# Two-layer token mixer on one core: mixtures, taps and norm moved beside the sparse heads, new rates for the Strassen groups

## The chip, the cores and the metric

The kernel runs on one core of one Trainium2 chip. The metric is the device time of one execution in microseconds (us), as the median of several runs. The core's engines are named as the profile names them: PE is the matrix engine, PEld its weight load, DVE the vector engine, ACT the scalar engine, POOL and SP the two others, of which SP issues most transfers and POOL the paced ones.

## The reference, cut to what matters

Two layers (D_MODEL 2048, 256 tokens) each normalise the input, multiply it by one wide matrix, run three mixers on the parts, gate them, project each back and add them under sigmoid gates:

```
h = rms_norm(x, norm_w)
proj = h @ w_in          # (256, 2048) @ (2048, IN_WIDTH)
(qa, ka, va, za, qi, ki, wi, ub, zb, qc, kc, vc, zc, gates) = split(proj)
y_a = (dsa_attention(rope(qa), rope(ka), va, rope(qi), rope(ki), wi, top_k) * silu(za)) @ w_a_out
y_b = (conformer_conv(ub, conv_w, conv_b, cln_w, cln_b) * silu(zb)) @ w_b_out
y_c = (stick_breaking_attention(qc, kc, vc) * silu(zc)) @ w_c_out
g = sigmoid(gates).reshape(b, s, 3, D_MODEL)
x + (g[..., 0, :] * y_a + g[..., 1, :] * y_b + g[..., 2, :] * y_c) @ w_out
```

All data are float32. The convolution has 31 taps per channel and is followed by a layer norm.

## The kernel before, in words

**Units.** Weights come from DRAM in pieces of 512 KB (256 rows by 512 columns), called units here; SP issues each load (L276) into one of six buffers `raw`. Each float32 operand is split in two numbers that the fast matrix mode takes: ACT rounds the unit (L287, `wh`), DVE subtracts to get the rest (L292, `wl`), with three buffers for each. PE then makes twelve matmuls for the unit (L303), eight with `wh` and four with `wl`. A chunk of 512 output columns is eight units in one PSUM tile (`acc`).

**Strassen groups.** Part of the merge gates (`gates`, four of the six column pairs named in `FAST`, L38) is computed by a Strassen scheme, `strassen`, one group after the other. A group works through "products" of six matmuls each, four with `wh` and two with `wl`, but each still wants a whole L287 and L292; 20 products make up its first part, with three sums of operands per five products (L1205, DVE), and eight its second. A group holds two tiles `mm` and one half of an `acc` tile: the banks o1 and o7 are in one `mm` tile. Between the parts the first results are read out of PSUM: L1256 (ACT), L1257 to L1260 (DVE); L1259 reads o7. The second part then adds on to o1 and o7 and ends in L1271 and L1272.

**What sets the order.** The emission order is made by Python generators at build time. After every unit, `background` (L156) advances the generators in two lists, `turns` and `stages`: at most `pace` and `wide` of them, sorted by rank and due time. The taps of the convolution are in a list of their own that gives one tap every `every` units. `combine` (L1135) yields the rest of the projection and the three back projections (za, zb, two `early` chunks, w_b, w_c, w_a); for each unit it adds RATES[kind] to a debt `owed`, and as long as `stages` is empty the debt is paid with items of the Strassen groups (one item is about a product). In `stages` are the indexer's two parts, four sparse heads, `conv_norm` (the layer norm of the convolution) and `mixtures` (L1070s to L1090s: DVE forms four sums of the activations for the groups, L1081 and L1089, and splits them, L416 and L417). Groups cannot start before all of these are done.

**Turns.** A gating that needs its data with rows and columns exchanged goes through `turn_in`: ACT copies the words apart (L180), SP issues two transposing DMAs (L186, the tuple `turn` says after how many units), DVE and ACT copy the words back (L194, L196), and a DVE chain (L447, L456) ends it. LATE is the tuple of the two za and the two zb gatings of a layer.

**Parked parts.** Half-done activations of w_c and w_a lie in DRAM (`parked`) and come back through POOL, one paced transfer after the other (L254, L256).

Of the kernel before, what the change touches and what calls it, by code (L numbers as in the profile page):

```python
# [12 lines left out]
ALU = mybir.AluOpType  # L13
# [16 lines left out]
EPS = 1e-6  # L30
NEG = -1e30
TAKEN = -3e38
RATES = (2.35, 2.35, 2.35, 2.35)
TURN = (8, 8)
EARLY = (4, 6)
LATE = (6, 6)
MERGED = ((3, 7), (3, 6), (3, 5))
FAST = ((2, 0), (2, 1), (0, 0), (0, 1))  # L38
SCALE = float(128 ** -0.5)
# [14 lines left out]
def trunk(ctx: ExitStack, tc: tile.TileContext, x, xt, w_in, w_a, w_b, w_c, w_out,  # L54
# [45 lines left out]
    def big():  # L100
        return [slot(), slot()]
# [34 lines left out]
    def t4(dt=F32):  # L136
        return tp.tile([P, 1024], dt, tag="t4", bufs=8, name=nm("t4"))
# [36 lines left out]
    def turn_in(src, dst, then=None, slots=True, turn=TURN, early=False):  # L174
        own, cols = words(slots)
        rows = own.rearrange("p (t w d) -> p t w d", t=NT, w=2)
        s16 = src.bitcast(U16).rearrange("p t (d w) -> p t d w", w=2)
        with tc.high_priority():
            for i in range(2):
                nc.scalar.copy(rows[:, :, i, :], s16[:, :, :, i])  # L180

        def steps():
            yield turn[0]
            with tc.high_priority() if turn in MERGED else nullcontext():
                for t in range(NT):
                    nc.sync.dma_start(cols.rearrange("p (g t) -> p g t", g=8)[:, :, t * P:(t + 1) * P],  # L186
                                      own[:, t * 1024:(t + 1) * 1024], transpose=True)
            yield turn[1]
            halves_ = cols.rearrange("p (w f t) -> p w f t", w=2, f=4)
            into = own.bitcast(F32).rearrange("p (f t) -> p f t", f=4) if dst is None else dst  # L190
            d16 = into.bitcast(U16).rearrange("p f (t w) -> p f t w", w=2)
            bound = turn == LATE or turn in MERGED
            with tc.issue_after(lows[0].ins) if bound else nullcontext(), tc.high_priority() if bound else nullcontext():
                nc.vector.tensor_copy(d16[:, :, :, 1], halves_[:, 1])  # L194
            with tc.issue_after(highs[0].ins) if bound else nullcontext(), tc.high_priority() if bound else nullcontext():
                (nc.vector.tensor_copy if early else nc.scalar.copy)(d16[:, :, :, 0], halves_[:, 0])  # L196
            more = None
            if dst is None:
                more = then(into, cols.bitcast(F32).rearrange("p (f t) -> p f t", f=4))
            elif then is not None:  # L200
                more = then()
            if hasattr(more, "send"):
                yield from more

        entry = [steps(), count[0], lambda: True, 0]
        turns.append(entry)
        advance(entry)
        return entry

    def start(gen, ready=lambda: True, rank=0):  # L210
        stages.append([gen, 0, ready, rank])
        return stages[-1]
# [5 lines left out]
    every = [1]  # L218
    pace = [1]
# [310 lines left out]
    for layer in range(DEPTH):  # L530
# [408 lines left out]
        def index_far(qb2=qb2, ki=ki, wi=wi, bias=bias):  # L939
            cb = cst[:, C_CB:C_CB + S]  # L940
            sc = tp.tile([P, S], F32, tag="sc", bufs=2, name=nm("sc"))
            bs = tp.tile([P, S], F32, tag="bias", bufs=2, name=nm("bias"))
            for g in range(NIH // 4):
                ps = mm_tile()
                complete(rotated[g])
                for q in range(4):
                    for n, (i, j) in enumerate(three):
                        nc.tensor.matmul(ps[:, q * S:(q + 1) * S], qb2[i][:, g * 4 + q, :], ki[:, j, 0, :],  # L948
                                         start=n == 0, stop=n == 2)
                rl = t4()  # L950
                nc.scalar.activation(rl, ps, AF.Relu)
                yield 1
                for q in range(4):
                    hd = g * 4 + q
                    nc.vector.scalar_tensor_tensor(sc, rl[:, q * S:(q + 1) * S], wi[:, 1, hd:hd + 1],
                                                   cb if hd == 0 else sc, op0=ALU.mult, op1=ALU.add)
            yield 1
            yield from chosen(sc, bs, cb)
            bias[1] = bs

        every[0] = 3
        start(index_far())
# [2 lines left out]
        def early_steps(b, j):  # L965
            a = yield from chunk_steps(w, [(O_G + b * D + j * 512, 512)], hx, KD)
            sg_ = t4().rearrange("p (t d) -> p t d", t=NT)
            with tc.high_priority():
                for t in range(NT):
                    nc.scalar.activation(sg_[:, t, :], a[t], AF.Tanh, scale=0.5)  # L970
            nc.gpsimd.dma_start(gates[b][:, :, j * 512:(j + 1) * 512].rearrange("t p d -> p t d"), sg_)  # L971
# [104 lines left out]
        def mixtures():  # L1076
            for h in range(2):
                f = []
                for u in range(2):
                    v = t4().rearrange("p (k t) -> p k t", k=4)  # L1080
                    nc.vector.tensor_add(v, hx[2 * u + h][:, :, 0, :].bitcast(F32), hx[2 * u + h][:, :, 1, :].bitcast(F32))  # L1081
                    f.append(v)
                (a11, a21), (a12, a22) = ((v[:, :, :P], v[:, :, P:]) for v in f)
                m1, m2 = (t4().rearrange("p (n k t) -> p n k t", n=2, k=4) for _ in range(2))
                yield 1
                for n, (o, x_, y_, op) in enumerate((
                        (m1[:, 0], a21, a22, ALU.subtract), (m1[:, 1], m1[:, 0], a11, ALU.subtract),
                        (m2[:, 0], a12, m1[:, 1], ALU.add), (m2[:, 1], a11, a21, ALU.subtract))):
                    nc.vector.tensor_tensor(o, x_, y_, op=op)  # L1089
                    split(mix[n][:, 4 * h:4 * h + 4, 0, :], mix[n][:, 4 * h:4 * h + 4, 1, :], o)  # L1090
                    yield 1

        start(mixtures(), rank=1)
        pace[0] = 2
        gated = {2: gate(O_ZC, qcT, [], w, hx, park=parked[2], slots=(True, False))}
        gated[0] = []
        za = gate_steps(O_ZA, qaT, [], w, hx, gated[0], park=parked[0], slots=(False, False), turn=LATE, need=sparse)
# [37 lines left out]
        def combine():  # L1135
            kind[0] = 2
            yield from za
            yield from early_steps(1, 2)
            yield from early_steps(1, 3)
            finish()  # L1140
            pace[0], wide[0] = 1, 2
            yield from zb
            mg.extend(v.rearrange("p a b -> p (a b)").rearrange("p (j t d) -> p j t d", j=2, t=NT) for v in big())
            for e in gated[1]:
                complete(e)
# [68 lines left out]
        def strassen(b, jj):  # L1214
# [50 lines left out]
            for u in range(4):  # L1265
                product(o1, plain(0, KC), u, halves(block(KC, 0, u)), True)
                yield 1
                product(o7, plain(1, KC), u, halves(kept[u]), True)
                yield 1
            with tc.high_priority():  # L1270
# [159 lines left out]
```

## Time and profile before

| | |
|---|---|
| runs, not profiled | 2059.34 us median of 3 (2058.57 to 2060.51) |
| the profiled execution | 2063.1 us, span in its trace 2061.2 us |
| PE busy | 2004.9 us, 97% of the span |
| DVE busy | 1650.7 us, 80% |
| ACT busy | 1435.9 us, 70% |
| POOL busy | 212.8 us, 10% |
| transfers | 475.39 MB, mean 231 GB/s |

The share of an engine is an average over stages that have different limits, so the table says which engine is full in most of them, not what ends a wait in one of them. The profiled execution's own time is 1.9 us above its span and 3.8 us above the median of the other runs. Times in the trace are in us from the start of its span.

### The profile page before, as it was taken

To read this page: it belongs to the slowest core of one execution; us is meant where nothing else is said; L and a number is where in the kernel's file an instruction comes from. 1 tells how busy PE (TensorE), PEld (TensorE's weight loads), DVE (VectorE), ACT (ScalarE), POOL (GpSimd) and SP (SyncE) were. 2 spreads that over 40 slices of the span, in tenths; PEclk is the share of its full clock that TensorE was granted. 3 is DMA by queue.
4 is the path that set the end of the run, shared out by engine and by line. 5 is a ranking of instruction groups with operands and counts; after the bars stand their busy time and mean duration, and the time that the engine had idled before them with its cause. 6 is when DMAs were issued, how large, how long until landed. Compare 5 with 4: busy or idle time off the path is not lost.

```text
span 2061.2 us, 27065 instructions
## 1 busy us (share of the span) xinstructions
PE 2004.9 (97%) x9470; PEld 1679.4 (81%) x9470; DVE 1650.7 (80%) x1792; ACT 1435.9 (70%) x2056; POOL 212.8 (10%) x252
## 2 busy tenths in 40 slices
PE   9999999999889989999999999999998899899998
PEld 7888889988668867887888888899886687778877
DVE  8688777897988777886676888788989887788765
ACT  7699877668766655565657997776787656565753
POOL 0000000000212113410000000000002211144000
PEclk9999999999999999999999999999999999999999
DMA  8787657669799889998977775586696998899973
GB/s 279 214 227 208 186 156 223 204 181 232 200 255 277 232 238 283 313 301 234 266 196 221 212 213 172 165 230 187 197 242 180 276 282 223 244 296 310 310 235 126
DMA packets 353145, 475.39 MB, mean 231 GB/s; under 512 B 109680, under 2 KB 167792, under 8 KB 352880
## 3 DMA queue, kind: packets, MB, share of 16 engines
q1 hardware_dynamic: 322688, 412.43, 68.5%
q0 software_dynamic: 28864, 58.73, 11.6%
q10 hardware_dynamic: 1456, 2.51, 0.4%
q8 instruction: 74, 1.21, 0.2%
q14 instruction: 63, 0.52, 0.1%
HBM read 423.79 MB, written 23.07 MB: 217 GB/s over the span
## 4 chain that ended last, share of the span: by engine, by line
PE 85%; DVE 5%; ACT 3%; DMA 3%; issue 2%; SPq 0%; POOL 0%; ACTq 0%; DVEq 0%; POOLq 0%
PE acc L303 73%; PE mm L303 9%; ACT wh L287 2%; DVE wl L292 2%; DMA t<-t 2%; DVE t L1205 1%; DVE s L1205 1%; DMA raw<-in_w_in_dram 1%; PE mm L948 1%; PE mm L978 1%; DMA s<-parked 0%; PE mm L1018 0%; PE mm L813 0%; PE mm L769 0%; ACT t L180 0%
## 5 line engine op out<-in xcount | busy, mean ns | idle before, releaser
L303 PE MATMUL acc<-wh,s 128*128 128x512 f32 (+2 forms) x4352 | 1071.5, 387 | 16.6 <-ACT wh L287 11.0
L292 DVE TENSOR_TENSOR wl<-raw,wh 128x1024 fp32r<-128x1024 f32 (+2 forms) x698 | 838.3, 1207 | 289.5 <-ACT wh L287 271.3
L287 ACT CAST wh<-raw 128x1024 fp32r<-128x1024 f32 (+2 forms) x697 | 723.6, 1040 | 394.3 <-PE acc L303 302.7
L303 PEld LDWEIGHTS acc<-wh,s 128*128 128x128 f32 x4352 | 804.0, 188 | 185.9 <-ACT wh L287 16.5
L303 PE MATMUL acc<-wl,s 128*128 128x512 f32 (+2 forms) x2176 | 576.1, 385 | 4.4 <-DVE wl L292 4.4
L303 PEld LDWEIGHTS acc<-wl,s 128*128 128x128 f32 x2176 | 403.8, 188 | 87.6 <-DVE wl L292 6.7
L303 PE MATMUL mm<-wh,s 128*128 128x512 f32 x768 | 214.7, 399 | 20.9 <-ACT wh L287 16.0
L482 ACT ACTIVATE t<-s,cst 128x255 f32<-128x255 f32 (+14 forms) x480 | 201.5, 489 | 0.1
L303 PEld LDWEIGHTS mm<-wh,s 128*128 128x128 f32 x768 | 145.2, 191 | 60.5 <-ACT wh L287 24.9
L254 POOL COPY sm<-sm 128x3 f32<-128x3 f32 x108 | 110.3, 1045 | 391.7 <-ACT sm L253 391.7
L485 DVE TENSOR_TENSOR s<-s,t 128x1020 f32<-128x1020 f32 (+14 forms) x120 | 138.5, 1154 | 2.0 <-ACT t L482 1.3
L303 PE MATMUL acc<-s,wh 128*128 128x384 f32 (+1 forms) x608 | 126.4, 348 | 0.0
L303 PE MATMUL mm<-wl,s 128*128 128x512 f32 x384 | 121.0, 396 | 4.6 <-DVE wl L292 4.3
L971 POOL DMA_DIRECT2D gates<-t x8 | 6.0, 752 | 1026.8 <-ACT t L970 1026.8
L303 PEld LDWEIGHTS acc<-s,wh 128*128 128x128 f32 x608 | 104.3, 189 | 3.1
L287 ACT CAST wh<-t 128x1024 fp32r<-128x1024 f32 x64 | 67.0, 1048 | 50.9 <-PE acc L303 16.2
L287 ACT CAST wh<-s 128x1024 fp32r<-128x1024 f32 x64 | 67.1, 1049 | 50.7 <-DVE s L1205 32.5
L292 DVE TENSOR_TENSOR wl<-s,wh 128x1024 fp32r<-128x1024 f32 x64 | 78.2, 1222 | 18.4 <-ACT wh L287 16.6
L292 DVE TENSOR_TENSOR wl<-t,wh 128x1024 fp32r<-128x1024 f32 x64 | 78.3, 1223 | 17.8 <-ACT wh L287 16.6
L303 PEld LDWEIGHTS mm<-wl,s 128*128 128x128 f32 x384 | 72.6, 191 | 23.7 <-DVE wl L292 8.9
L303 PEld LDWEIGHTS acc<-s,wl 128*128 128x128 f32 x608 | 79.2, 191 | 1.0
L303 PE MATMUL acc<-s,wl 128*128 128x192 f32 (+1 forms) x608 | 79.7, 273 | 0.0
(248 smaller groups left out, 1361.8 us busy)
## 6 DMA issues: line engine op xcount, KB each, us to landing
raw<-in_w_in_dram SPq DMA_DIRECT2D x554, 512.0 KB, 4.5
raw<-in_w_out_dram SPq DMA_DIRECT2D x64, 512.0 KB, 5.0
s<-in_w_in_dram POOLq DMA_DIRECT2D x32, 512.0 KB, 9.1
raw<-in_w_b_dram SPq DMA_DIRECT2D x32, 512.0 KB, 5.5
raw<-in_w_c_dram SPq DMA_DIRECT2D x32, 512.0 KB, 6.7
raw<-in_w_a_dram SPq DMA_DIRECT2D x32, 512.0 KB, 7.1
t<-gates POOLq DMA_DIRECT2D x20, 512.0 KB, 7.0
s<-parked POOLq DMA_DIRECT2D x32, 256.0 KB, 6.4
```

The lines of the kernel that those rows point to most:

```text
L254: seen = nc.gpsimd.tensor_copy(copy[:, :3], mark)
L287: highs[0] = nc.scalar.copy(u[1], u[0])
L292: sub = nc.vector.tensor_sub(u[2], u[0], u[1].bitcast(F32))
L303: newest[0] = nc.tensor.matmul(o, lhsT, rhs, start=start, stop=stop, skip_group_check=True)
L482: nc.scalar.activation(o[:, i, :S - d], yT[:, c, :S - d], AF.Copy, scale=wq)
L485: sums.append(lambda: nc.vector.tensor_add(to, to, o[:, :, :S - d]))
L948: nc.tensor.matmul(ps[:, q * S:(q + 1) * S], qb2[i][:, g * 4 + q, :], ki[:, j, 0, :], start=n == 0, stop=n == 2)
L971: nc.gpsimd.dma_start(gates[b][:, :, j * 512:(j + 1) * 512].rearrange("t p d -> p t d"), sg_)
L978: nc.tensor.matmul(ps[:, q * n:(q + 1) * n], qaT[:, c * 4 + q, ts_], kaT[:, c, :n], start=True, stop=True)
L1205: nc.vector.tensor_tensor(o, a_, b_, op=op)
```

## The change

Five things change. (1) `mixtures` forms its sums in place in the four operand tiles and asks for no further buffers; it starts as soon as the indexer's second part has ended, with rank 0, ahead of the sparse heads, and from there on `pace` is 3 (was 2), `wide` 6 (was 4) and `every` 1 (was 3), so that the rest of the taps comes with every unit. (2) RATES is 2.15 for kind 2 (za, zb and early) and 2.5 for kinds 0 and 1 (the back projections); it was 2.35. (3) The transposing DMAs of LATE are emitted with high priority, and the wait of units behind them is 8 (was 6). (4) The two `early` chunks stand behind zb (were ahead of it), and `finish()` ahead of zb. (5) The second part of a group makes its four o1 products and then its four o7 products (they alternated).

```diff
-RATES = (2.35, 2.35, 2.35, 2.35)
+RATES = (2.5, 2.5, 2.15, 2.5)
-LATE = (6, 6)
+LATE = (6, 8)
...
-            with tc.high_priority() if turn in MERGED else nullcontext():
+            with tc.high_priority() if turn == LATE or turn in MERGED else nullcontext():
...
             bias[1] = bs
+            bias["far"] = True
...
-                m1, m2 = (t4().rearrange("p (n k t) -> p n k t", n=2, k=4) for _ in range(2))
...
-                        (m1[:, 0], a21, a22, ALU.subtract), (m1[:, 1], m1[:, 0], a11, ALU.subtract),
-                        (m2[:, 0], a12, m1[:, 1], ALU.add), (m2[:, 1], a11, a21, ALU.subtract))):
+                        (a22, a21, a22, ALU.subtract), (a22, a22, a11, ALU.subtract),
+                        (a12, a12, a22, ALU.add), (a21, a11, a21, ALU.subtract))):
...
-        start(mixtures(), rank=1)
-        pace[0] = 2
+        start(mixtures(), lambda: "far" in bias, 0)
+        pace[0], wide[0], every[0] = 3, 6, 1
...
             yield from za
-            yield from early_steps(1, 2)
-            yield from early_steps(1, 3)
             finish()
             pace[0], wide[0] = 1, 2
             yield from zb
+            yield from early_steps(1, 2)
+            yield from early_steps(1, 3)
...
                 product(o1, plain(0, KC), u, halves(block(KC, 0, u)), True)
                 yield 1
+            for u in range(4):
                 product(o7, plain(1, KC), u, halves(kept[u]), True)
                 yield 1
```

Three places in the order of instructions follow, all of layer 0 (layer 1 is the same). The first is PE where the first Strassen group runs. In these rows `mm_5100`, `mm_5101` and `acc_5102` are the group's banks before, and `mm_4876`, `mm_4877` and `acc_4878` after; `acc_4832` is a chunk of 512 columns. Before:

```order
L303 MATMUL mm_5100<-wh_5243,s_9_100 128x512 x4
L303 MATMUL mm_5101<-wh_5253,s_686_4130 128x512
L303 MATMUL mm_5100<-wl_5244,s_9_100 128x512 x2
L303 MATMUL mm_5101<-wh_5253,s_686_4130 128x512 x3
L303 MATMUL mm_5101<-wl_5254,s_686_4130 128x512 x2
L303 MATMUL mm_5101<-wh_5267,s_687_4131 128x512 x4
L303 MATMUL acc_5102<-wh_5279,s_688_4132 128x512 x2
L303 MATMUL mm_5101<-wl_5268,s_687_4131 128x512 x2
L303 MATMUL acc_5102<-wh_5279,s_688_4132 128x512 x2
L303 MATMUL mm_5100<-wh_5294,s_689_4133 128x512
L303 MATMUL acc_5102<-wl_5280,s_688_4132 128x512 x2
L303 MATMUL mm_5100<-wh_5294,s_689_4133 128x512 x3
```

After:

```order
L303 MATMUL acc_4832<-wh_4994,s_10_101 128x512 x8
L303 MATMUL acc_4832<-wl_4995,s_10_101 128x512 x4
L303 MATMUL mm_4876<-wh_5014,s_8_99 128x512 x4
L303 MATMUL mm_4876<-wl_5015,s_8_99 128x512 x2
L303 MATMUL mm_4877<-wh_5024,s_686_4130 128x512 x4
L303 MATMUL mm_4877<-wl_5025,s_686_4130 128x512 x2
L303 MATMUL acc_4832<-wh_5039,s_10_101 128x512 x8
L303 MATMUL acc_4832<-wl_5040,s_10_101 128x512 x4
L303 MATMUL mm_4877<-wh_5057,s_687_4131 128x512 x4
L303 MATMUL mm_4877<-wl_5058,s_687_4131 128x512 x2
L303 MATMUL acc_4832<-wh_5070,s_11_102 128x512 x8
L303 MATMUL acc_4832<-wl_5071,s_11_102 128x512 x4
```

Before, products follow products (six matmuls each) without a unit between them; after, a unit of twelve matmuls stands behind every one or two of them.

The second place is DVE at the end of the first part of the fourth group, while w_a is being multiplied; `acc_7792` before and `acc_7762` after is w_a's first chunk, and L1169 multiplies it by its merge gate. Before:

```order
L292 TENSOR_TENSOR wl_7902<-raw_7899,wh_7901 128x1024
L1257 TENSOR_TENSOR t_1532_7872<-mm_7244,t_1532_7872 128x512
L1258 TENSOR_TENSOR t_1533_7873<-mm_7244,t_1532_7872 128x512
L292 TENSOR_TENSOR wl_7912<-s_1396_7311,wh_7911 128x1024
L1259 TENSOR_TENSOR t_1533_7873<-t_1533_7873,mm_7243 128x512
L1260 TENSOR_TENSOR t_1533_7873<-acc_7245,t_1533_7873 128x512
L1169 SCALAR_TENSOR_TENSOR t_1513_7786<-t_1513_7786,acc_7792 128x1024
L292 TENSOR_TENSOR wl_7937<-raw_7935,wh_7936 128x1024
L292 TENSOR_TENSOR wl_7956<-raw_7953,wh_7955 128x1024
L292 TENSOR_TENSOR wl_7966<-s_1423_7432,wh_7965 128x1024
L1173 TENSOR_TENSOR s_1173_6405<-s_1173_6405,t_1513_7786 128x1024
```

After:

```order
L292 TENSOR_TENSOR wl_7923<-raw_7921,wh_7922 128x1024
L1257 TENSOR_TENSOR t_1531_7886<-mm_7313,t_1531_7886 128x512
L1258 TENSOR_TENSOR t_1532_7887<-mm_7313,t_1531_7886 128x512
L1169 SCALAR_TENSOR_TENSOR t_1502_7756<-t_1502_7756,acc_7762 128x1024
L292 TENSOR_TENSOR wl_7942<-raw_7939,wh_7941 128x1024
L1173 TENSOR_TENSOR s_1150_6340<-s_1150_6340,t_1502_7756 128x1024
L1259 TENSOR_TENSOR t_1532_7887<-t_1532_7887,mm_7312 128x512
L1260 TENSOR_TENSOR t_1532_7887<-acc_7314,t_1532_7887 128x512
```

L1169, the subtraction behind it and L1173 now stand between L1258 and L1259; before, one subtraction stood there, and L1169 came behind L1260. On PE the chunk's last matmuls stand directly ahead of the first product of the group's second part in the order after, which asks for L1259.

The third place is DVE at the last gating of zb: its back copy L194, then the chain L447 and L456 that writes the second half of what w_b multiplies by. Before, `raw_6479`, `raw_6509` and `raw_6558` are units of w_b; their subtractions stand among the gating's operations:

```order
L292 TENSOR_TENSOR wl_6481<-raw_6479,wh_6480 128x1024
L292 TENSOR_TENSOR wl_6498<-s_1193_6477,wh_6497 128x1024
L1205 TENSOR_TENSOR t_1199_6507<-raw_6397,raw_6475 128x1024
L292 TENSOR_TENSOR wl_6511<-raw_6509,wh_6510 128x1024
L194 COPY t_1171_6401<-t_1172_6402 128x1024
L292 TENSOR_TENSOR wl_6528<-raw_6475,wh_6527 128x1024
L447 SCALAR_TENSOR_TENSOR t_1171_6401<-t_1172_6402,s_81_537 128x1024
L292 TENSOR_TENSOR wl_6543<-t_1199_6507,wh_6542 128x1024
L1205 TENSOR_TENSOR t_1211_6556<-raw_6552,raw_6554 128x1024
L292 TENSOR_TENSOR wl_6560<-raw_6558,wh_6559 128x1024
L292 TENSOR_TENSOR wl_6577<-raw_6552,wh_6576 128x1024
L456 TENSOR_TENSOR s_1176_6417<-t_1171_6401,s_1176_6417 128x4x256
```

After, the same three operations of this gating stand among units of the early chunks and the second group, and the first unit of w_b is the twelfth row behind this piece:

```order
L194 COPY t_1027_5766<-t_1028_5767 128x1024
L292 TENSOR_TENSOR wl_6119<-raw_6091,wh_6118 128x1024
L292 TENSOR_TENSOR wl_6129<-t_1100_6095,wh_6128 128x1024
L1205 TENSOR_TENSOR s_1109_6140<-t_1100_6095,raw_6138 128x1024
L292 TENSOR_TENSOR wl_6144<-raw_6142,wh_6143 128x1024
L447 SCALAR_TENSOR_TENSOR t_1027_5766<-t_1028_5767,s_81_537 128x1024
L292 TENSOR_TENSOR wl_6162<-s_1109_6140,wh_6161 128x1024
L1205 TENSOR_TENSOR t_1115_6171<-raw_6093,raw_6138 128x1024
L292 TENSOR_TENSOR wl_6175<-raw_6173,wh_6174 128x1024
L292 TENSOR_TENSOR wl_6194<-raw_6138,wh_6193 128x1024
L292 TENSOR_TENSOR wl_6210<-raw_6208,wh_6209 128x1024
L456 TENSOR_TENSOR s_1119_6191<-t_1027_5766,s_1119_6191 128x4x256
```

Before, w_b's first unit stands eleven rows ahead of L194; after, w_b's first unit stands 23 rows behind it.

## Rows read from the trace of the kernel before

**Rows 1.** The page: busy time, share and instructions; chain by engine.

```profile
PE 2004.9 (97%) x9470; PEld 1679.4 (81%) x9470; DVE 1650.7 (80%) x1792; ACT 1435.9 (70%) x2056; POOL 212.8 (10%) x252
...
PE 85%; DVE 5%; ACT 3%; DMA 3%; issue 2%; SPq 0%; POOL 0%; ACTq 0%; DVEq 0%; POOLq 0%
```

**Rows 2.** Windows: engines' busy time (count of instructions), PEclk, DMA share, GB/s.

```profile
450.00:500.00 50.00, 50.00 (x223) 41.52 (x222) 37.81 (x42) 43.74 (x79) 0.00 (x0) 1.00 0.86 222
500.00:550.00 50.00, 50.00 (x223) 41.39 (x222) 48.45 (x59) 40.61 (x47) 1.52 (x2) 1.00 0.82 211
545.00:612.00 67.00, 54.57 (x211) 40.34 (x211) 59.65 (x58) 43.29 (x54) 21.21 (x13) 0.95 0.83 228
715.00:760.00 45.00, 38.42 (x154) 29.38 (x152) 34.93 (x33) 27.42 (x36) 13.42 (x16) 0.92 0.85 227
...
1565.00:1635.00 70.00, 57.20 (x229) 42.59 (x229) 63.92 (x62) 47.91 (x59) 20.86 (x13) 0.98 0.85 227
1738.00:1785.00 47.00, 40.66 (x165) 30.96 (x164) 36.72 (x33) 27.92 (x33) 12.46 (x15) 0.96 0.89 234
```

**Rows 3.** Groups by line and shape on DVE: busy us, mean ns, idle before.

```profile
L292 DVE TENSOR_TENSOR wl<-raw,wh 128x1024 fp32r<-128x1024 f32 x678 | 824.1, 1222 | 271.7 <-ACT wh L287 257.8 <-ACT t L779 10.0
...
L1205 DVE TENSOR_TENSOR t<-raw,raw 128x1024 f32<-128x1024 f32 x64 | 77.9, 1218 | 0.0
...
L1169 DVE SCALAR_TENSOR_TENSOR t<-t,acc 128x1024 f32<-128x1024 f32 x16 | 19.5, 1218 | 4.6 <-PE acc L303 4.6
...
L1259 DVE TENSOR_TENSOR t<-t,mm 128x512 f32<-128x512 f32 x8 | 5.4, 680 | 0.0
```

**Rows 4.** The chain that ended last, 545 to 612: start, us, what.

```profile
590.49 2.72 PE acc L303 x12
...
600.04 1.06 ACT wh L287
601.13 1.23 DVE wl L292
602.36 0.61 DVE t L1259
```

**Rows 5.** Waits of PE: us in total, times, longest us.

```profile
PE mm L303 <- DVE t L1259: 4.9, 3, 2.2
```

**Rows 6.** The chain that ended last, 715 to 760: start, us, what.

```profile
722.44 1.82 ACT t L180 x2
...
725.62 8.39 DMA t<-t
...
734.10 0.75 DVE t L194
...
736.40 2.93 PE acc L303 x6
...
756.76 1.36 PE mm L303 x6
```

**Rows 7.** Groups by line and shape on ACT.

```profile
L196 ACT COPY t<-t 128x1024 uint16<-128x1024 uint16 x19 | 25.7, 1354 | 23.1 <-DMA t<-t 23.1
L180 ACT COPY t<-acc 128x1024 uint16<-128x1024 uint16 x24 | 23.2, 1009 | 2.0 <-DVE t L1089 2.0
```

**Rows 8.** The chain that ended last, 796 to 812.

```profile
801.60 4.67 DMA s<-parked
```

**Rows 9.** Windows with a low granted clock or much traffic.

```profile
735.00:740.00 5.00, 3.60 (x9) 2.84 (x10) 3.62 (x4) 4.78 (x7) 2.44 (x2) 0.50 0.63 215
605.00:610.00 5.00, 5.00 (x17) 3.94 (x17) 2.45 (x2) 1.84 (x3) 0.00 (x0) 0.72 1.13 383
850.00:900.00 50.00, 49.94 (x220) 40.98 (x219) 42.08 (x39) 29.86 (x42) 22.46 (x30) 1.00 1.06 319
```

**Rows 10.** Waits of SP's queue.

```profile
SPq L186 <- ACT wh L287: 38.1, 21, 3.7
```

## The prediction

> **What bounds the kernel now.** I read the page first: PE is busy 97% of the span, DVE 80%, and the chain that ended last runs through PE for 85% [rows 1]. So time can only be won where PE stands still or waits between matmuls, and the next question is where. I counted matmuls per stretch, since a matmul that waits for its operand can show as busy. Two stretches at full speed have 223 matmuls in 50 us each, which is 50 / 223 = 0.2242 us per matmul, and there DVE is busy 37.8 and 48.5 us of 50 [rows 2]. What a stretch lasts above its count times 0.2242 us I call lost.
>
> Stretch 545 to 612, where the mixtures end and the first Strassen group runs: 211 matmuls are worth 47.3 us of 67, so 19.7 us are lost. Its like in layer 1, 1565 to 1635: 70 - 229 x 0.2242 = 18.7. Stretch 715 to 760, where zb ends and w_b begins: 45 - 154 x 0.2242 = 10.5; in layer 1, 1738 to 1785: 47 - 165 x 0.2242 = 10.0 [rows 2]. These 58.9 us are nearly all that is to be had; the rest of the loss is single gaps such as one of 4.67 us of a parked load's transfer on the chain, in which PE had work for most of it [rows 8].
>
> The first pair is a DVE bound. A unit costs PE 2.72 us [rows 4] and DVE one subtraction of 1.222 us; a product costs PE 1.36 us [rows 6] and DVE the same 1.222, plus three sums of 1.218 us per five products [rows 3], 1.95 us in all. Products in a row therefore outrun DVE by 0.6 us each. Before, 13 stand in a row (a part of them is the first order piece), because the groups wait for all stages while the debt in `owed` grows, and the mixtures' own DVE work is just ahead.
>
> To see whether this arithmetic gives the measured loss, I took DVE's instructions from the last subtraction that had to wait for a buffer of PE to L1259, which PE waits for at the end of the group's first part, each at its row's duration: 43 subtractions (52.5), 12 sums (14.6) and 44.2 us of mixtures, norm and gating make 111.3 us. PE's matmuls in the same piece of the program (20 products, 22 units) make 91.7. The excess is 19.6 us, and 19.7 are lost. The method holds, so I use it for the order after.
>
> The second pair is the end of zb. The chain goes through ACT's two copies L180, a transposing transfer of 8.39 us, the back copy L194, and only then PE [rows 6]; meanwhile w_b's first units stand behind the back copy in DVE's and ACT's order.
>
> **The change part by part.** *First group.* The change starts the mixtures beside the sparse heads, so the taps and the mixtures spread over units with 2.72 us of PE each, and groups begin 11 units sooner (counted in the two orders) with a debt that makes no burst (units stand between products in the order after). The same count, from the last waiting subtraction to L1259: 59 subtractions (72.1), 12 sums (14.6), 64.4 us of others (more taps and heads are now within it), 151.1 us; PE's matmuls 141.5. The excess is 9.6 us, of which 2.66 us are the tail at L1259 (a subtraction, a back copy L194 of 0.75 [rows 6] and L1259 of 0.68 us [rows 3] now stand between the last product and the next). So 19.7 becomes 9.6 and 18.7 becomes 9.8: **-10.1 and -8.9 us**. The bounds: if the heads' own dependence chains stop PE as well, nothing is won here; if DVE's excess is eaten by slack ahead of the piece (DVE idles a quarter of 450 to 500 [rows 2]), all of 19.
>
> *zb to w_b.* With two early chunks and parts of group 2 between, 16 units lie between zb's end and w_b, over 40 us of PE work against a transfer of 8.39. The 10.5 and 10.0 us go. In their place PE meets a chain of ACT where early begins: L180 twice (1.01 us each), L196 (1.35) [rows 7] and casts, against which PE has too little stored: I work out 2.0 us from these durations. **-8.5 and -8.0**. Bounds: 0 to 4 us for the new wait.
>
> *End of the fourth group.* Here the order costs. In the second order piece L1169 waits for the end of w_a's chunk, and L1259 comes behind it; PE stands from the chunk's end until L1259 is done: 1.218 + 1.222 + 1.218 + 0.680 = 4.3 us [rows 3]. Before, one subtraction stood there and PE had a product and a unit to do. Passing from engine to engine adds 0.3. Gaps of such length were followed by a granted clock of 0.5 (the 1.2 GHz level) from 735 to 740 [rows 9]; half speed for 3.4 us takes 1.7, and I put in half of that. **+5.5 in each layer**; bounds 3 and 7.
>
> *Second part.* Four o1 products in a row load 512 KB per 1.36 us, which is 385 GB/s. Windows reach 383 for 5 us but only 319 over 50 us with a DMA share above 1 [rows 9]. Six buffers carry part of it. At 319 GB/s four loads need 6.6 us against 5.4 of PE, 1.2 us too many per group at the worst, nothing at the best; I take 0.3, as buffers are full at the start: **+2.4** for eight groups. The four o7 products load nothing, and give that back to the queue.
>
> *Parked loads.* Rate 2.5 in the back projections brings w_c's first units up to four units sooner to their parked parts, paced by POOL. A transfer of 4.67 us stood on the chain before [rows 8]; sooner by some 3 us of PE work, part of it hidden: **+1 per layer**, bounds 0 and 3.
>
> *At nothing.* Rate 2.15: all groups end at the same unit in both orders. The mixtures in place: same operations on DVE, no new wait on a tile used elsewhere. The LATE transfers' high priority: on SP they wait for ACT's copies, and the weight load behind each would itself wait for DVE's subtraction of a unit further on, so nothing is held; this cover is gone if SP comes to them before ACT has copied (third rival).
>
> The Trainium skill, on "PSUM — Partial Sum Buffer" (section Terms), puts the collision of two engines on a bank, not on a tile. By that rule alone a product into o1 could run while DVE reads o7, and the new order (all o1 first) would free PE for four products: the 4.3 us would not be paid. The trace has PE waiting 4.9 us in three cases on L1259 [rows 5], and the product that waits there before is an o1 product too; the wait is written for the tile. So the rule does not set the sum. It would give 2039.3 - 11 - 5 = about 2024, and is a rival below.
>
> **Sum.** Layer 0: -10.1 - 8.5 + 5.5 + 1 = -12.1; layer 1: -8.9 - 8.0 + 5.5 + 1 = -10.4; second parts +2.4. Together -20.1. The profiled execution took 2063.1 us (span 2061.2, 1.9 beside it), so 2043.0; it stood 3.8 above the median of the runs shown, 2059.3, so 2039.2. As the unknown costs (bursts of loads, clock, parked loads) reach further up than down, I take 2041.
>
> **The rivals.** (1) *The stall moves.* If in the sparse heads' stretch PE waits for chains between DVE and ACT rather than for DVE's sum, the mixtures among them lengthen each chain. For it: DVE is busy 97% in 500 to 550 already [rows 2], with PE still full, so the reserve ends there. Against it: the arithmetic gave the measured loss without any chains. If half of the 19 stays, 2041 + 9.5 = 2050; if all stays, 2060.
>
> (2) *Loads become the bound in the second parts.* At 1.2 us for each of eight groups, and as much again where the queue is still behind at the end, 2041 + 10 = 2051.
>
> (3) *Slower: SP is held.* The 16 transposing DMAs of LATE now stand ahead of weight loads on SP, which works in order. SP waited for ACT's work at such a DMA up to 3.7 us [rows 10]. There are two for each of four gatings per layer, so eight pairs. If each pair holds the loads by 3 us more than six buffers cover, 8 x 3 = 24 us eat the whole gain and the time is about 2065; it decides from 3.1 us per pair on (20.1 + 4.1 over eight). Against: loads behind them wait for later subtractions anyway.
>
> (4) *Banks are waited for apart*: 2024, as above.
>
> (5) *The change does nothing at the first group*, since groups that start sooner have less time for what they need: as the second half of (1), 2060.
>
> **How the numbers follow.** A change of 0.2%, 4.1 us, is about what a measurement of this kernel can tell from none. My forecast (2034 to 2047) has 0.60; half the stall stays 0.12; the loads 0.11; all of the stall stays, alone or with (5), 0.07; SP is held 0.06; banks apart 0.04. The likeliest gives 2041. The range 2034 to 2053 holds the forecast, the half stall and the loads, 0.83 in all, and leaves the two-sided rest out; its low end is the sum with the parked and load terms at nothing and the clock term gone (2039.2 - 2 - 2.4 - 1.7 = 2033). Faster by more than 4.1 us: 0.60 + 0.12 + 0.11 + 0.04 and a part of the others' edge, less some doubt, 0.85; within it 0.08; slower 0.07.
>
> **What would show it.** In the changed kernel's windows the stretch from the sparse heads to the first group's end should lose some 10 us, without a run of products; the transposing transfer of zb should be off the chain, with no gap near w_b's start; a gap of 4 to 5 us should stand ahead of the fourth group's second part in each layer, released by L1259, new; PE's waits for L1259 should grow from 4.9 to about 13 us. In the second parts PE should wait on `raw` by under 1 us per group. I am wrong if the heads' stretch shows more idle PE than the 9.6 us, if SP's waits at L186 are followed by waits of PE for casts of a late load, or if the gap at the fourth group is missing.

## The result, and the profile after

The changed kernel takes 2079.64 us (median of 4 runs, 2076.08 to 2082.95) against 2059.49 before: ratio 1.0097, 95% interval 1.0079 to 1.0116. It is 20 us slower where I forecast 18 us less. The profiled execution took 2078.2 us with a span of 2076.4, 15.2 above the span before.

From the page of the changed kernel come the busy times, the chain by engine, and one row of DMA issues (KB each, median us from issue to landing):

```profile
PE 2009.5 (97%) x9470; PEld 1687.5 (81%) x9470; DVE 1646.1 (79%) x1792; ACT 1436.4 (69%) x2056; POOL 223.4 (11%) x252
...
PE 86%; DMA 6%; DVE 4%; ACT 3%; issue 1%; SPq 0%; POOL 0%; ACTq 0%; DVEq 0%; POOLq 0%
...
s<-parked POOLq DMA_DIRECT2D x32, 256.0 KB, 10.6
```

PE is as busy as before [rows 1], but transfers have grown on the chain from 3% to 6%, and the parked parts take 10.6 us to land (6.4 on the page of before). The windows of the changed kernel stand for the places that the prediction names (columns as in [rows 2]):

```profile
455.00:562.00 107.00, 101.01 (x433) 81.05 (x431) 98.73 (x110) 90.21 (x127) 20.87 (x6) 0.98 0.78 204
562.00:592.00 30.00, 29.36 (x129) 24.11 (x130) 25.88 (x24) 18.26 (x20) 7.96 (x8) 1.00 1.20 302
592.00:610.00 18.00, 13.11 (x49) 10.34 (x48) 9.21 (x12) 10.75 (x12) 0.00 (x0) 0.81 0.99 282
610.00:650.00 40.00, 38.48 (x170) 31.45 (x169) 32.67 (x29) 27.46 (x32) 9.17 (x12) 1.00 0.83 241
780.00:805.00 25.00, 19.28 (x71) 15.03 (x70) 14.65 (x14) 10.69 (x21) 10.84 (x20) 0.80 1.00 308
870.00:912.00 42.00, 35.27 (x143) 27.98 (x142) 29.09 (x27) 20.93 (x25) 6.01 (x7) 0.92 1.04 309
1612.00:1640.00 28.00, 22.46 (x91) 17.88 (x90) 16.18 (x17) 15.81 (x17) 1.41 (x2) 0.94 0.98 294
1810.00:1835.00 25.00, 19.05 (x71) 14.92 (x70) 14.86 (x15) 10.37 (x21) 10.93 (x20) 0.86 0.96 296
1921.00:1940.00 19.00, 14.35 (x52) 11.32 (x51) 12.15 (x13) 9.90 (x12) 1.59 (x2) 0.82 0.87 254
```

Lost time is counted as in the prediction, at 0.2242 us per matmul; in the heads' stretch the count is off by some us, as matmuls of other sizes are among them.

| lost, us | before, layer 0 / 1 | changed | predicted |
|---|---|---|---|
| heads to the first group's end (after: 455 to 610) | 19.7 / 18.7 | 18.0 / 17.5 | 9.6 / 9.8 |
| zb to w_b (after: in 610 to 650) | 10.5 / 10.0 | 1.9 / 1.9 | 2.0 |
| start of w_c (after: 780 to 805) | 1.4 / 1.2 | 9.1 / 9.1 | 1 more |
| end of the fourth group (after: 870 to 912; 1890 to 1940) | under 1.4 | 9.9 / 12.8 | 5.5 more |

The four lines of both layers come to some 16 us more than before; the spans differ by 15.2. The second line came out as worked out. The other three did not, and the waits of PE name two things that ended them:

```profile
PE mm L303 <- DVE t L1259: 19.4, 4, 5.2
PE acc L303 <- DMA s<-parked: 11.7, 4, 5.4
```

Waits for L1259 rose from 4.9 us [rows 5] to 19.4, where I expected about 13, and parked parts, which PE hardly waited for, cost 11.7 us in four waits. At the first group's end, the chain (start, us, what) runs so:

```profile
582.33 12.00 DMA raw<-in_w_in_dram
...
596.66 0.70 DVE t L1257
...
599.20 0.65 DVE t L194
599.85 0.58 DVE t L1259
...
600.56 2.90 PE mm L303 x6
```

A load took 12.0 us to land; its cast and subtraction stand ahead of L1257 on DVE, and PE, with nothing else to do, starts again after L1259. At the fourth group's end:

```profile
894.82 0.69 DVE t L1257
...
896.15 1.21 DVE t L1169
...
898.50 1.14 DVE s L1173
...
899.63 0.61 DVE t L1259
...
900.38 2.90 PE mm L303 x6
```

This is the gap of 4.3 us that the prediction worked out from the order (L1169, a subtraction, L1173, L1259 in a row). It is there: PE waits 5.2 us in layer 0 and 4.6 in layer 1. The rest of the 9.9 us of layer 0 stands beside it. Behind the gap the granted clock is at the 1.2 GHz level:

```profile
900.00:905.00 5.00, 4.62 (x11) 3.69 (x12) 2.15 (x3) 3.64 (x5) 0.00 (x0) 0.50 1.19 331
```

Eleven matmuls in these 5 us are 2.5 us lost, where I had put in 0.85; and 1.4 us ahead of the gap PE waits for the cast of a load of w_a that landed late. At the start of w_c:

```profile
788.06 9.16 DMA s<-parked
...
797.27 8.64 PE acc L303 x25
```

The transfer of a parked part takes 9.16 us; its like before took 4.67 [rows 8].

### The profile page after: what moved, and what is told of

The parts are those of the page before. It is cut to its first block, busy times and chain, and to the rows that moved or that the text cites. A ratio compares the mean times of both kernels' runs of the same rounds, so it can differ in the third digit from the quotient of the medians.

```text
span 2076.4 us, 27053 instructions
## 1 busy us (share of the span) xinstructions
PE 2009.5 (97%) x9470; PEld 1687.5 (81%) x9470; DVE 1646.1 (79%) x1792; ACT 1436.4 (69%) x2056; POOL 223.4 (11%) x252
## 4 chain that ended last, share of the span: by engine, by line
PE 86%; DMA 6%; DVE 4%; ACT 3%; issue 1%; SPq 0%; POOL 0%; ACTq 0%; DVEq 0%; POOLq 0%
PE acc L303 71%; PE mm L303 11%; DMA raw<-in_w_in_dram 2%; DVE wl L292 2%; DMA t<-t 2%; ACT wh L287 1%; DMA raw<-in_w_a_dram 1%; DMA s<-parked 1%; PE mm L948 1%; PE mm L979 1%; PE mm L813 0%; PE mm L769 0%; ACT t L1000 0%; DVE s L1205 0%; PE mm L1019 0%
## 5 line engine op out<-in xcount | busy, mean ns | idle before, releaser
L303 PE MATMUL acc<-wh,s 128*128 128x512 f32 (+2 forms) x4352 | 1078.7, 389 | 20.8 <-DMA s<-parked 11.7
L303 PE MATMUL mm<-wh,s 128*128 128x512 f32 x768 | 210.9, 396 | 29.9 <-DVE t L1259 19.4
L254 POOL COPY sm<-sm 128x3 f32<-128x3 f32 x108 | 129.8, 1356 | 404.2 <-ACT sm L253 404.1
L303 PEld LDWEIGHTS mm<-wl,s 128*128 128x128 f32 x384 | 73.0, 191 | 16.5 <-DVE wl L292 1.3
L1205 DVE TENSOR_TENSOR t<-raw,raw 128x1024 f32<-128x1024 f32 x64 | 77.9, 1217 | 2.4 <-DMA raw<-in_w_in_dram 2.4
## 6 DMA issues: line engine op xcount, KB each, us to landing
s<-parked POOLq DMA_DIRECT2D x32, 256.0 KB, 10.6
```

Of the source, the lines that this page charges most:

```text
L254: seen = nc.gpsimd.tensor_copy(copy[:, :3], mark)
L303: newest[0] = nc.tensor.matmul(o, lhsT, rhs, start=start, stop=stop, skip_group_check=True)
L1205: nc.vector.tensor_tensor(o, a_, b_, op=op)
```

## The experiments

Every edit below is made to the changed kernel, if not said otherwise; "good rates" are 2.25 for kind 2 and 2.5 for kinds 0 and 1. Nothing is left out of the computation in any of them.

**1. One part undone at a time.** Four kernels: the second part's products alternate again (alt); RATES of before (rates); LATE of before (late); the early chunks ahead of zb (early).

```diff
                 yield 1
-            for u in range(4):
                 product(o7, plain(1, KC), u, halves(kept[u]), True)
```

```diff
-RATES = (2.5, 2.5, 2.15, 2.5)
+RATES = (2.35, 2.35, 2.35, 2.35)
```

```diff
-LATE = (6, 8)
+LATE = (6, 6)
...
-            with tc.high_priority() if turn == LATE or turn in MERGED else nullcontext():
+            with tc.high_priority() if turn in MERGED else nullcontext():
```

```diff
+            yield from early_steps(1, 2)
+            yield from early_steps(1, 3)
             finish()
             pace[0], wide[0] = 1, 2
             yield from zb
-            yield from early_steps(1, 2)
-            yield from early_steps(1, 3)
```

> The changed kernel with the o1 and o7 products of the second part alternating again. Theory A (late loads: at the ends of groups 1 and 4 weight loads land 12 to 13.7 us after issue, because four loads in a row meet full DMA engines, and DVE's reads of the banks stand behind the subtraction of the late unit): the stretches 592 to 610, 870 to 912, 1612 to 1640 and 1890 to 1940, which lose 7.0, 9.9, 7.6 and 12.8 us in the changed kernel, lose half of it, so 12 to 18 us less in all, near 2063. Theory B (the place of L1259 behind other DVE work alone makes the gap): under 3 us of difference, 2077 to 2080. The wait for parked parts (two stretches of 9.1 us) stays by either.

> The changed kernel with RATES of before (2.35 for all kinds). Theory C (rate 2.5 brings w_c to its parked parts before POOL and the transfers have brought them): the two stretches of 9.1 us before w_c lose 2 us each, 14 us less, and the fourth group's end loses less as its L1259 no longer meets the end of w_a's chunk: 2055 to 2065. Theory A (transfers crowd because of the second part's order) sees little here: 2073 to 2079. The first group's end stays, unless 2.15 had spread it.

> The changed kernel with the LATE turns as before: transposing DMAs not ahead, six units of wait. Theory D (my third rival: SP is held, or the transposing transfers, moved ahead, fill the DMA engines where the first group's loads come): at least 8 us less, 2070 or below, with the first group's end losing under 4 us. Theory A: no gain, 2077 to 2082, or a loss, as the back copies then wait for the transfers.

> The changed kernel with the two early chunks ahead of zb again. If the move of the early chunks is what took the stall of 10 us out of the change from zb to w_b, it comes back in both layers, 16 to 20 us, near 2097. If the LATE priority alone took it away, the time stays, 2075 to 2082. The wait for parked parts stays by either, as w_b lies between.

Measured: alt 2075.56 (2071.71 to 2081.17; ratio to before 1.0071, 1.0052 to 1.009), rates 2037.07 (0.9889, 0.9872 to 0.9905), late 2084.73 (1.0111), early 2087.33 (1.0125). Of the four, only rates is clear of the changed kernel's own interval (1.0079 to 1.0116); the differences of the other three, 4 us less, 5 and 8 us more, are not clear of noise. Theory A, on which I had set most, fell: alternating brings at most some 4 us, not 12 to 18, and the waits for L1259 stay (19.5 us). For early the 16 to 20 us did not come. Undoing one line of numbers brings 42.6 us, which no expectation had. The page of the kernel with RATES of before:

```profile
PE 1996.9 (98%) x9470; PEld 1680.8 (83%) x9470; DVE 1646.0 (81%) x1792; ACT 1436.5 (71%) x2056; POOL 232.1 (11%) x252
```

The same 9470 matmuls keep PE busy for 12.6 us less than in the changed kernel, at a mean granted clock of 0.994 against 0.987, and span less busy time is 37.6 us against 66.9. So, as an estimate, some 29 us of the 42 between the two spans are PE standing still, and some 13 the slower clock. The windows:

```profile
455.00:562.00 107.00, 101.42 (x435) 81.46 (x433) 98.72 (x111) 90.65 (x128) 20.90 (x6) 0.98 0.78 205
562.00:592.00 30.00, 29.36 (x130) 23.94 (x129) 27.04 (x24) 17.95 (x21) 11.97 (x8) 1.00 1.18 309
592.00:610.00 18.00, 18.00 (x80) 14.63 (x79) 14.60 (x15) 15.80 (x18) 0.53 (x1) 1.00 0.79 286
610.00:650.00 40.00, 37.93 (x167) 31.02 (x166) 34.26 (x31) 26.76 (x33) 10.87 (x14) 1.00 1.01 280
775.00:805.00 30.00, 27.34 (x107) 21.67 (x106) 18.81 (x18) 15.58 (x25) 8.81 (x18) 0.89 0.88 292
870.00:900.00 30.00, 27.69 (x123) 22.59 (x122) 23.37 (x23) 18.10 (x21) 2.73 (x4) 1.00 1.09 333
```

Heads and first group lose 9.5 + 0.9 + 0.1 = 10.4 us there (455 to 562, 562 to 592, 592 to 610), zb 2.6, the start of w_c 6.0, the fourth group's end 2.4; and its waits (us in total, times, longest):

```profile
PE acc L303 <- DMA s<-parked: 5.1, 2, 2.6
PE mm L303 <- DVE t L1259: 4.5, 2, 2.3
```

So with RATES as they were, the sizes that I predicted at the first group (9.6) and at zb (2.0) are nearly there. The stretch 592 to 610, which had lost 7.0, runs at full speed. But the place is not all as predicted. Most of the 9.5 us of the heads' stretch is lost in two pieces:

```profile
480.00:500.00 20.00, 17.43 (x70) 13.66 (x69) 16.41 (x20) 15.79 (x24) 0.00 (x0) 0.91 1.06 237
520.00:540.00 20.00, 16.98 (x72) 12.78 (x71) 19.44 (x20) 16.92 (x21) 6.37 (x2) 1.00 0.66 177
```

From 520 to 540 DVE is full while the first products run, as my sum had it, and 3.9 us are lost. From 480 to 500 DVE is not full, and 4.3 us are lost: PE waits there for ACT's L1039 of a sparse head, once per layer, and the granted clock falls behind it.

```profile
PE mm L1045 <- ACT ph L1039: 5.2, 2, 2.8
```

The kernel before has no such wait. It is a chain of the kind of my first rival, and my sum of DVE's work did not hold it.

**2. Is it the rate or the place?** In PE's order of the changed kernel one unit stands between the last product of the first group's first part and the first of its second part; with RATES of before there are two:

```
changed:                                             RATES of before:
MATMUL mm_4876<-wl_5400,s_689_4133  x2               MATMUL mm_4876<-wl_5382,s_689_4133  x2
MATMUL acc_5171<-wh_5410,s_11_102   x8               MATMUL acc_5171<-wh_5392,s_11_102   x8
MATMUL acc_5171<-wl_5411,s_11_102   x4               MATMUL acc_5171<-wl_5393,s_11_102   x4
MATMUL mm_4876<-wh_5438,s_10_101    x4               MATMUL acc_5171<-wh_5419,s_11_102   x8
                                                     MATMUL acc_5171<-wl_5420,s_11_102   x4
                                                     MATMUL mm_4876<-wh_5438,s_10_101    x4
```

The reason is in the generators. The read-out (L1256 to L1260) is emitted when the debt allows; in the changed kernel this falls on the last unit of a chunk for groups 1 and 4. The next chunk needs the bank that the group still holds until L1260, and the next product the tile that L1259 reads: so after one unit PE has nothing that it may do. Theory P (phase): what costs is a read-out with less than two units of the running chunk behind the last product. Theory R: rate 2.5 itself is too dense. Three kernels tell them apart, with a fourth for the gain of the first part of the change.

In the order r225_25 (as dense as the changed kernel behind zb), r225_235 (nowhere denser than before), owed1 (the changed rates, the debt starting at 1) and r_mix (the last edit below, together with RATES 2.35 for all kinds):

```diff
-RATES = (2.5, 2.5, 2.15, 2.5)
+RATES = (2.5, 2.5, 2.25, 2.5)
```

```diff
-RATES = (2.5, 2.5, 2.15, 2.5)
+RATES = (2.35, 2.35, 2.25, 2.35)
```

```diff
-        owed = 0
+        owed = 1
```

```diff
-        start(mixtures(), lambda: "far" in bias, 0)
-        pace[0], wide[0], every[0] = 3, 6, 1
+        start(mixtures(), rank=1)
+        pace[0] = 2
```

> RATES 2.25 for kind 2 and 2.5 for kinds 0 and 1, all else as changed. Theory P (phase: a group's read-out costs when it falls on the last unit of a chunk, since the next chunk's bank and the group's own banks then wait for the same DVE reads; in the changed kernel this holds for groups 1 and 4, here for none): as the run with 2.35, 2033 to 2045. Theory R (rate 2.5 in the back projections is itself too much for DVE, the loads or the parked parts): 2062 to 2080.

> RATES 2.25 for kind 2 and 2.35 for kinds 0 and 1, so no rate above that of before; but the read-outs of groups 3 and 4 fall on chunk ends. Theory P: four read-outs at 5 to 9 us each, 2055 to 2072, with gaps of PE waiting for L1259 at groups 3 and 4 and none at group 1. Theory R: 2034 to 2044.

> The changed kernel's rates, with the debt starting at 1 instead of 0, which moves read-outs by a unit: group 3 falls on a chunk end, groups 1 and 4 no longer. Theory P: the 7.0, 7.6 us at group 1 and most of 9.9, 12.8 us at group 4 go and one stall per layer comes at group 3, just ahead of w_c: 2050 to 2068. Theory R: 2074 to 2084.

> RATES 2.35 and the first part of the change undone (mixtures start after the taps with rank 1, pace 2, wide 4, every 3; in place still). The stretch to the first group's end should lose 19 us per layer again instead of 10.4: my first two terms, 8.9 and 10.1, so 2037 + 17 to 19, 2053 to 2058. If it stays under 2045, the gain of the kernel with rates of before comes from elsewhere.

Measured: r225_25 2031.76 (0.9863, 0.9844 to 0.9883), r225_235 2051.15 (0.9949), owed1 2057.63 (0.9986), r_mix 2063.08 (1.001, 0.9993 to 1.0027). Rate 2.5 behind zb is the fastest so far, and 2.35 there with the same 2.25 ahead of it is 19 us slower; a start of the debt at 1 takes 22 us off at the same rates. Theory R is out. Theory P has the order right but not each size: r225_25 came out 1 us below its range and r225_235 4 us below, as its read-outs made PE wait 3.8 and 4.6 us where I had 5 to 9. owed1 has its waits at groups 3 and 4:

```profile
PE mm L303 <- DVE t L1259: 21.8, 4, 7.6
```

That corrected my count: for its fourth group the read-out is not on a chunk's end but one unit ahead of it, and one unit of the chunk is left as well. Counted as units between the two parts in PE's order, the kernels line up (a unit of which only the first two to four matmuls stand there is counted as one; last column: PE's waits for L1259, total us, times, longest; layer 1 has the same counts; the last three rows hold runs of the next two parts too):

| kernel | units between, groups 1 to 4 | waits for L1259 |
|---|---|---|
| before | 2, 2, 2, 2 | 4.9, 3, 2.2 |
| changed; alt; early; late | 1, 2, 3, 1 | 19.4, 4, 5.2; 19.5, 4, 5.0; 20.0, 4, 5.6; 18.2, 4, 4.9 |
| rates | 2, 3, 2, 2 | 4.5, 2, 2.3 |
| r225_25 | 2, 3, 2, 2 | 4.6, 2, 2.6 |
| r225_235 | 2, 3, 1, 1 | 16.9, 4, 4.6 |
| owed1 | 2, 3, 0, 1 | 21.8, 4, 7.6 |
| b_rates | 1, 3, 3, 1 | 15.6, 4, 4.6 |
| a_unpark | 1, 2, 2, 1 | 19.0, 4, 4.9 |
| r_mix; g_alt; g_early; g_late; g_unpark | 2, 2 or 3, 2, 2 | 7.6, 3, 2.8; 3.3, 2, 2.0; 4.2, 2, 2.2; 8.2, 4, 3.1; 1.7, 2, 1.3 |

Two or three units: no wait for L1259 over 3.1 us, and that one in g_late (one of 3.2 us at such a place in r_mix is put down to L180). One or none: four waits in a run, 3.9 us each on average in b_rates (the shortest 2.9), 4.9 in the changed kernel, up to 7.6 in owed1. At the fourth group the waits of rates and r225_25, 2.0 to 2.6 us with two units, are about one unit (2.72 us of PE) shorter than the 4.6 and 5.2 of the changed kernel with one. r_mix lost 26 us against rates where I had 17 to 19 for the first two terms; its runs spread from 2056.62 to 2070.19, so the terms are confirmed in sign and about in size.

**3. The terms by themselves.** At good rates, where no read-out makes PE wait for more than 2.6 us, each remaining part was undone again, and RATES alone were put into the kernel before (b_rates).

> The kernel before with the changed RATES (2.5, 2.5, 2.15) alone. The read-outs of groups 1 and 4 fall on chunk ends as in the changed kernel. Theory P: the fourth group's end loses 8 to 12 us per layer, the start of w_c 5 to 8, the first group's end 2 to 4 more than before: 2090 to 2105. If the rates hurt only together with the other parts of the change: 2055 to 2066.

> RATES 2.25 and 2.5 (no read-out on a chunk's end), second parts alternating again. My term for four o1 products in a row was +2.4 us: if it holds, 2027 to 2031 here; if the order of banks helps, as the run at the changed kernel's rates hinted by -4 the other way with a wide interval, over 2034.

> RATES 2.25 and 2.5, the early chunks ahead of zb again. My term for this was 8.5 and 8.0 us: 2046 to 2050 if it is the move alone that takes the stall from zb to w_b away. If the LATE priority takes half of it, as 7.7 us at the changed kernel's rates say: 2037 to 2042.

> RATES 2.25 and 2.5, LATE as before. My third rival (transposing transfers ahead on SP hold the loads) would gain here, 2024 or below; at nothing, as I costed it, 2029 to 2035; if the earlier issue is what brings the back copies in time, 2035 to 2042.

Measured: b_rates 2079.38 (1.0091, 1.0076 to 1.0106), g_alt 2030.62 (0.9852, 0.9831 to 0.9873), g_early 2065.95 (1.0021, 1.0011 to 1.003), g_late 2038.93 (0.9891, 0.9876 to 0.9906). The rates alone cost the kernel before 17 us, less than the 30 or more that I expected, but with the same two waits:

```profile
PE mm L303 <- DVE t L1259: 15.6, 4, 4.6
...
PE acc L303 <- DMA s<-parked: 11.4, 4, 5.4
```

Undoing the order of banks (g_alt) brings 1 us, 2030.62 against 2031.76, within the runs' spread; that is in the range that I gave for my +2.4, which is neither shown nor excluded. LATE (the transfers ahead and the wait of 8 units together) wins 7 us; my third rival had the wrong sign. The early chunks win 34, twice the 16.5 of my two terms; a chain of g_early shows what they cover:

```profile
714.23 9.60 DMA t<-t
...
723.91 0.82 ACT t L196
...
725.11 1.05 ACT s L454
...
726.21 9.96 PE acc L303 x36
```

```profile
PE acc L303 <- ACT s L454: 26.8, 2, 14.1
```

With the early chunks ahead of zb, PE waits 13 to 14 us per layer for L454, behind a transfer of 9.60 us, and no product is left to do. At the changed kernel's rates the same edit cost some 8 us at most, since products of the second group were still left there. What the move is worth depends on this, which I had not worked out; neither of my two ranges for g_early held.

**4. The parked parts.** The edit asks for w_c's parked parts ahead of w_b's last chunk, at the changed rates (a_unpark) and at good rates (g_unpark).

```diff
                 if n == 1:
-                    gx = unpark(2)
+                    gx = early2
                 for j in range(4):
+                    if n == 0 and j == 3:
+                        early2 = unpark(2)
```

> The changed kernel with the parked parts of w_c asked for ahead of w_b's last chunk, eight units sooner, as those of w_a are. Where the late transfers of the parked parts cause the two stretches of 9.1 us before w_c, these shrink to under 2.5 us: 2062 to 2068. If the stretch is set by something else at the seam (the read-out of group 3 inside w_c's first units), it stays: 2074 to 2082.

> The same in the kernel with RATES 2.25 and 2.5: the stretches at w_c lose 2.4 and 4.2 us there, so 4 to 6 us less, 2026 to 2028, if the transfers are the cause; otherwise 2030 to 2034.

Measured: a_unpark 2069.69 (1.0043, 1.0027 to 1.006), 10 us less than the changed kernel, where the best that I expected was 2062 to 2068; g_unpark 2025.3 (2022.26 to 2028.09; 0.9829, 0.9814 to 0.9844), the fastest of all. The windows of g_unpark at the three places:

```profile
592.00:610.00 18.00, 18.00 (x81) 14.90 (x80) 14.70 (x15) 14.28 (x16) 0.00 (x0) 1.00 1.12 323
770.00:800.00 30.00, 30.00 (x133) 24.66 (x133) 22.85 (x21) 19.45 (x29) 10.92 (x20) 1.00 0.98 317
865.00:900.00 35.00, 33.11 (x145) 26.63 (x144) 25.85 (x25) 21.06 (x24) 0.91 (x2) 1.00 1.00 298
```

The start of w_c has 133 matmuls in 30 us, so nothing is lost there. PE has no wait for parked parts left in g_unpark. In a_unpark 3.9 us stay of 9.1 in layer 0, so the transfers' start is the larger part; what the rest is (the read-out of group 3 stands among w_c's first units there) was not tried apart. The waits at groups 1 and 4 stay in a_unpark, as its counts say (L1261 is the L1259 of the other kernels, as the edit adds two lines):

```profile
PE mm L303 <- DVE t L1261: 19.0, 4, 4.9
```

## Why the prediction was wrong

The step that failed is one sentence under "At nothing": "Rate 2.15: all groups end at the same unit in both orders." In PE's order it does not hold: counted in units, the second parts of groups 1 to 4 end 2, 3, 2 and 1 units later in the changed kernel than before, in both layers, and with RATES of before put back they end at the same units as before. So the rates also set at which unit of a chunk each group is read out, and I gave that no price, though I had the count at hand: I had worked out the gap at the fourth group from its order, took it for a single place and did not ask where the other read-outs fall. RATES alone cost 42.6 us in the changed kernel and 17 in the one before. They reach the time by two ways. Groups 1 and 4 are read out with one unit left. And w_c's parked parts are asked for late: in layer 0 of the changed kernel POOL issues the first of them 2.2 us after PE began w_b's last unit, and PE goes on 8.5 us after it; in r225_25 it is issued 0.7 us ahead of that unit, and PE goes on 6.0 us after it. Why POOL is later there was not tried.

Point by point. **First group** (-10.1, -8.9): the size was right, 10.4 us lost in layer 0 with RATES of before, but partly by luck: some 4 of them stand at a head's chain through ACT that the sum did not hold. (The 91.7 us of PE in the prediction's test of its method are more than the 20 products and 22 units named there, which make 87.0; matmuls of the heads are among them.) In the changed kernel the tail, put at 2.66 us, measured 7.0 and 7.6. I had taken its subtraction for ready, but its load landed 12.0 us after issue. **zb to w_b** (-8.5, -8.0): the stretch came out as worked out, -8.6 and -8.1, but undoing the move alone cost some 8 us in one kernel (not clear of noise) and 34 in another, so the term holds for this order only. **End of the fourth group** (+5.5): right in kind, mis-sized; 9.9 and 12.8. The wait was as worked out (5.2 and 4.6 against 4.3 + 0.3). The clock took more than the 0.85 put in, and waits for casts ahead of the gap, 1.4 and 2.8 us, were not in the term. **Second part** (+2.4): not clear of noise; the order after cost 1 us at good rates and 4 at the changed ones, both the way that I had it. **Parked loads** (+1): mis-sized; +7.7 and +7.9. PE waits 11.7 / 2 = 5.9 us per layer for them, and a low granted clock goes with the rest (0.80 from 780 to 805, 0.86 at its like in layer 1). Rate 2.5, which I gave as the reason, does not do it alone: r225_25 has it and waits 4.0 us for them in all. **LATE** at nothing: it wins 7 us at good rates; the 5 at the changed ones are not clear of noise.

Rivals: (1) did not happen in its size, as 10.4 shows, but its mechanism did once per layer, at L1045. (5) came near in size in the changed kernel, where 18.0 of 19.7 us stay, but not for its reason: with other RATES the same early start loses 10.4. (2) had the right kind of trouble, late loads, but at the ends of first parts; with the order of banks undone (alt) the waits there stayed. (3) was the side on which it ended, with another mechanism; LATE helps. (4), banks: the Trainium skill ("PSUM — Partial Sum Buffer", section Terms) puts a collision on the bank; here product and L1259 are in the same tile but in two banks, and PE waited up to 5.2 us for L1259 all the same, so what the program waits on sets the time, as the prediction had it.

Open: the counts in PE's order tell which read-outs stall, not why the first group's wait with one unit is 2.9 and 3.4 us in b_rates and 4.6 and 4.9 in the changed kernel; late loads are a likely part, which was not tried apart. Nor was the first part of the change taken apart (its start, rank, pace, width and taps were undone together).

## What to carry to other kernels

A number that paces background work sets a phase as well as a density: list, for the old and the new value, where each hand-over (a read-out, a bank given back) falls against the ends of the foreground's chunks, and count the work that the waiting engine still has there. A gap found in one place of a new order is a reason to count all places of its kind. Test a pacing number alone and next to its neighbours: four pairs of rates (ahead of w_b / behind) took 2079.6 (2.15 / 2.5), 2031.8 (2.25 / 2.5), 2051.2 (2.25 / 2.35) and 2037.1 us (2.35 / 2.35) here, without a trend.

## What the runs showed of the hardware that I had not expected

The DMA engines can be busier where they move fewer bytes, when many small packets are among them. In the changed kernel, at the first group's end (columns as in [rows 2]; DMA share and GB/s last), and the packets of the first of the two stretches:

```profile
580.00:590.00 10.00, 10.00 (x45) 8.17 (x44) 6.59 (x7) 4.85 (x6) 1.53 (x2) 1.00 1.25 289
590.00:600.00 10.00, 5.67 (x25) 4.32 (x24) 7.61 (x9) 7.00 (x9) 0.00 (x0) 0.91 1.07 349
DMA packets 3070, 2.89 MB, mean 289 GB/s; under 512 B 1471, under 2 KB 2186, under 8 KB 3069
```

The share is 1.25 with 289 GB/s, against 1.07 with 349 ten us later, where 110 of 1814 packets are under 512 B. Transposing transfers and stores of parked parts, issued between 570 and 580, are in flight beside the loads in the first stretch; which of them fills the engines was not tried apart. The load issued in that stretch took 12.0 us to land, where the median of such loads was 4.5. I had priced transfers by bytes alone.
